# Layer A's head outputs: scaling issued one step later, their transposes in one PSUM bank, v's transposes in the projections' three

## The chip, the cores and the metric

One core of a Trainium2 chip runs the whole program. The metric is the device time of one execution in microseconds (us); of the kernel before, three runs are at hand, and the median is given. The profile comes from a further execution of the same program.

The engines are TensorE (PE in the profile, with its weight loads as PEld), VectorE (DVE), ScalarE (ACT), GpSimd (POOL) and SyncE (SP), which issues the DMAs. TensorE writes its results into PSUM, a small memory with eight banks; the other engines read them from there.

## The reference, cut to what matters

The reference is one inference step of a two-layer decoder trunk on a prompt of 1024 tokens and on 8 sample tokens with a state of their own, all in float32. Layer B (a gated MLP over chunks) is not touched by the change. Layer A is a gated linear recurrence with 8 heads, keys of 128 and values of 256:

```python
proj = h @ w_in
q, f, i, z = jnp.split(proj, [D_MODEL, 2 * D_MODEL, 2 * D_MODEL + D_INNER], axis=-1)
q = jax.nn.silu(q)
logf = jnp.logaddexp(jnp.log(lbh), jnp.log1p(-lbh) + jax.nn.log_sigmoid(f))
k = -jnp.expm1(logf)
o, S = hgrn2_chunkwise(q, k, v=i, logf, s0)     # S_t = diag(f_t) S_{t-1} + k_t v_t^T,  o_t = S_t^T q_t
o = rmsnorm(o, g_norm).reshape(B, L, D_INNER)   # per head, over its 256 values
return (o * jax.nn.silu(z)) @ w_out, S
```

The change concerns the line with `rmsnorm` and the product with `silu(z)`: each head's output `o` comes out with tokens on the partitions, is scaled there by one number for each token, is transposed, and is multiplied by the gate.

## The kernel before

**The work.** The 1032 tokens lie in three chunks of 384, 384 and 264 columns (`W`; the last 8 columns of the third are the sample tokens). A product in float32 is made of three matmuls of shorter operands (lines L230, L231 and L232: high by high, low by high, high by low). A projection (`proj`) of one chunk to 128 outputs is 24 such matmuls into one bank, `ps_proj`. Layer A runs from about 200 to 765 us of the span; most of it is the loop over 8 heads.

For each head h, `head_proj` runs the projections f (three chunks, `fk`), q (three chunks, `qq`: ScalarE makes the sigmoid `sg` at L618, VectorE multiplies it with the projection into `qk` at L619), and v (two halves of 128 outputs by three chunks; ScalarE copies each to `vf` at L720). The last head projects its gate z as well; the other heads' gates were computed earlier and are read back as `zs`.

**The steps.** TensorE executes in the order in which the program is written. Beside the projections stand generators that a counter drives: `tk.tick()` is called in the middle and at the end of each projection and runs whatever has come due; `yield 4` in a generator means "go on four ticks later". A tick is thus half a projection of TensorE's work, about 2 us. The generators of a head are:

- `v_token_major`: transposes v's copy (`pt_v`, three transposes at L763) and splits it into a high part `vh` and a low part `vl` (L226, VectorE);
- `decay` (for each chunk): products of the forget gates on VectorE (L821 to L852), small matmuls (L802), and the transposes of k (`pt_k`, L866), which are split into `kh` and `kl`;
- `recur`: for each 128 tokens the matmuls into `pd` and `po`, the new state `S` (L919) with its parts `Sh` and `Sl`, and `out_sum`: `on` is the copy of the output (L881), and its sum of squares follows at L882;
- `finish` (for each chunk): `out_scale` adds the epsilon (`ss_e`, L888, VectorE) and takes the power -1/2 on GpSimd (`rsq`, L239); ScalarE scales the two or three `on` tiles of the chunk (L940); `OD[0]`, that is 4, ticks later TensorE transposes them (`pt_o`, L894), and VectorE multiplies each by the gate into `oz` (L947);
- `sample`: the sample tokens' states are updated (L981, L982), their outputs are summed into `pos` (L989), and they go the same way as `finish`: scaling at L995, `OD[1]` ticks, transposes (L998, issued at L894), and the product with the gate at L1003.

What a head begins, the next head's first 30 us finish: the output transposes of head h's chunks stand between the projections of head h+1.

The engines other than TensorE don't execute in written order. A scheduler sets their order when the program is built, and moves ahead what stands under `tc.high_priority`. In `finish` the product L947 stands under it, the scaling L940 doesn't.

**The banks.** The tiles in PSUM take a bank by their tag. Tag "mm" has three banks in rotation; "pt" has one. A tile that takes a bank waits until the last reader of the tile that held it is done. Before the change:

- "mm": `ps_proj`, `pt_k`, `pos`, the outputs' transposes `pt_o` of heads 0 to 6, and the sample's transposes of all heads;
- "pt": v's transposes `pt_v`, and the outputs' transposes `pt_o` of the last head;
- one bank each: `po` (tag "po"), `pD` (tag "pA"), `pC`, `pd`.

The functions that the change touches, and what calls them:

## Time and profile before

| | |
|---|---|
| median of 3 runs | 1887.39 us (1887.23 to 1890.06) |
| the profiled execution | 1887.56 us, span 1885.8 us |
| mean granted TensorE clock | 0.991 |
| TensorE busy | 1829.3 us, 97% of the span |
| VectorE busy | 1363.0 us, 72% |
| ScalarE busy | 895.5 us, 47% |
| GpSimd busy | 406.0 us, 22% |
| layer A's heads, 200 to 765 us: TensorE, VectorE, ScalarE, GpSimd busy | 536.37, 452.52, 325.25, 66.99 us of 565 |

The rows of the timeline read: start in us, duration in us, engine, line, operation, output and inputs with their sizes, the number of instructions that the row groups, and in brackets the idle time of the engine just ahead of it with what released it. Where a row groups several instructions, its duration runs from the first one's start to the last one's end. The rows of the waits read: waiting engine, tile and line, then the releaser, then total us, number of waits, the longest one. The rows of the windows give, for each stretch, its length, the busy time of PE, PEld, DVE, ACT and POOL (number of instructions in brackets), then the granted clock, the DMAs' share and their GB/s.

### The profile page before, as it was taken

Reading aid. Unit: us, or ns where it says so; the run is one execution under the profiler, and the core shown is the slowest. Engines: PE = TensorE matmul, PEld = TensorE weight load, DVE = VectorE, ACT = ScalarE, POOL = GpSimd, SP = SyncE. Lnnn points to the kernel's source line nnn. Section 1 sums busy time; section 2 is a strip of 40 time slices with the busy share of each in tenths; the row PEclk is TensorE's granted clock in tenths of the full one; section 3 lists DMA queues with packets and bytes.
Section 4 is the critical chain, followed back from the end, with each engine's and each line's share of the span. In section 5 each row is a group of like instructions: output and inputs, shape, how many; then the busy total and the mean of one; then the engine's idle time right before and its main releaser. Section 6 shows DMA issues by size and latency. Waiting matters only on the chain.

```text
span 1885.8 us, 37107 instructions
## 1 busy us (share of the span) xinstructions
PE 1829.3 (97%) x14458; PEld 1793.3 (95%) x14458; DVE 1363.0 (72%) x2760; ACT 895.5 (47%) x1905; POOL 406.0 (22%) x407
## 2 busy tenths in 40 slices
PE   8999999999999989999999999999999999999997
PEld 7999999998989988999999999999999998999997
DVE  6766788779778767678665855577777878777744
ACT  6533365556556546435344544433444345445342
POOL 4000011011111101000233333244544452000222
PEclk9999999999999989999999999999999999999999
DMA  6233334345444246954343343323334546953223
GB/s 218 78 111 104 110 117 126 115 135 168 157 127 128 86 138 193 309 175 134 95 138 112 115 143 90 101 79 109 117 112 156 180 132 195 305 177 113 72 91 113
DMA packets 164560, 258.11 MB, mean 137 GB/s; under 512 B 16096, under 2 KB 136864, under 8 KB 163360
## 3 DMA queue, kind: packets, MB, share of 16 engines
q1 hardware_dynamic: 164384, 255.74, 42.8%
q8 instruction: 113, 1.85, 0.4%
q14 instruction: 63, 0.52, 0.1%
HBM read 182.88 MB, written 72.80 MB: 136 GB/s over the span
## 4 chain that ended last, share of the span: by engine, by line
PE 72%; DVE 15%; DMA 5%; ACT 3%; issue 3%; POOL 2%; SPq 1%; DVEq 0%; POOLq 0%; ACTq 0%
PE ps_proj L230 17%; PE ps_proj L231 17%; PE ps_proj L232 17%; PE ps_d L230 3%; PE ps_d L232 2%; PE ps_d L231 2%; PE ps_o L230 2%; PE ps_o L231 2%; PE ps_o L232 2%; DMA vb<-vd 1%; DVE wlo L152 1%; POOL rsq L239 1%; DVE S L982 1%; PE psp L1513 1%; DVE M L821 1%
## 5 line engine op out<-in xcount | busy, mean ns | idle before, releaser
L230 PE MATMUL ps_proj<-bh,whi 128*128 128x264 f32 (+1 forms) x2248 | 718.6, 320 | 14.7 <-DVE qk L619 13.3
L231 PE MATMUL ps_proj<-bl,whi 128*128 128x264 f32 (+1 forms) x2248 | 703.2, 313 | 5.3 <-DVE bl L226 2.7
L232 PE MATMUL ps_proj<-bh,wlo 128*128 128x264 f32 (+1 forms) x2248 | 702.5, 313 | 1.2 <-DVE wlo L152 1.2
L230 PEld LDWEIGHTS ps_proj<-bh,whi 128*128 128x128 f32 x2248 | 425.6, 189 | 18.5 <-DVE qk L619 14.7
L231 PEld LDWEIGHTS ps_proj<-bl,whi 128*128 128x128 f32 x2248 | 426.1, 190 | 8.9 <-DVE bl L226 5.5
L232 PEld LDWEIGHTS ps_proj<-bh,wlo 128*128 128x128 f32 x2248 | 425.0, 189 | 2.1 <-DVE wlo L152 2.1
L152 DVE TENSOR_TENSOR wlo<-wstg,whi 128x1024 fp32r<-128x1024 f32 x148 | 184.9, 1249 | 114.2 <-ACT whi L151 113.7
L151 ACT CAST whi<-wstg 128x1024 fp32r<-128x1024 f32 x148 | 155.3, 1049 | 140.4 <-PE ps_proj L231 118.1
L151 ACT CAST shi<-ssum 128x512 fp32r<-128x512 f32 x152 | 94.1, 622 | 190.7 <-PE ps_proj L231 90.5
L152 DVE TENSOR_TENSOR slo<-ssum,shi 128x512 fp32r<-128x512 f32 x152 | 112.0, 739 | 10.4 <-ACT shi L151 10.0
L239 POOL TENSOR_TENSOR rsq<-rms_e,mhalf 128x3 f32<-128x3 f32 x15 | 17.8, 1188 | 360.1 <-DVE rms_e L284 360.1
L230 PE MATMUL ps_proj<-xmh,shi 128*128 128x384 f32 x244 | 83.2, 341 | 2.4 <-DVE sg L1529 1.3
L232 PE MATMUL ps_proj<-xmh,slo 128*128 128x384 f32 x244 | 81.7, 335 | 0.0
L231 PE MATMUL ps_proj<-xml,shi 128*128 128x384 f32 x244 | 81.7, 335 | 0.0
L852 DVE TENSOR_TENSOR qk<-qk,t 128x384 f32<-128x384 f32 (+1 forms) x144 | 74.0, 517 | 8.5 <-PE pC L802 7.3
L230 PE MATMUL ps_o<-bh,whi 128*128 128x384 f32 (+1 forms) x232 | 73.2, 316 | 0.0
L231 PE MATMUL ps_o<-bl,whi 128*128 128x384 f32 (+1 forms) x232 | 72.7, 313 | 0.0
L232 PE MATMUL ps_o<-bh,wlo 128*128 128x384 f32 (+1 forms) x232 | 72.7, 313 | 0.0
L1522 POOL TENSOR_TENSOR s<-s,u 128x384 f32<-128x384 f32 (+1 forms) x48 | 54.2, 1130 | 71.3 <-DVE s L1516 70.7
L1261 DVE TENSOR_TENSOR tmp<-tmp,pj 128x384 f32<-128x384 f32 (+1 forms) x48 | 25.6, 533 | 56.0 <-ACT tmp L1260 52.4
L239 POOL TENSOR_TENSOR rsq<-ss_e,mhalf 128x3 f32<-128x3 f32 (+2 forms) x32 | 27.8, 868 | 172.9 <-DVE ss_e L888 134.9
L266 POOL TENSOR_TENSOR ssq<-ssq,tmp 128x384 f32<-128x384 f32 (+1 forms) x36 | 34.2, 951 | 108.1 <-ACT tmp L265 108.1
(376 smaller groups left out, 4148.1 us busy)
## 6 DMA issues: line engine op xcount, KB each, us to landing
wstg<-in_wina SPq DMA_DIRECT2D x48, 512.0 KB, 3.9
wstg<-in_winb SPq DMA_DIRECT2D x48, 512.0 KB, 4.1
pj<-ppd SPq DMA_DIRECT2D x16, 516.0 KB, 4.8
S<-in_st SPq DMA_DIRECT2D x16, 512.0 KB, 4.7
vb<-vd SPq DMA_DIRECT2D x16, 512.0 KB, 4.9
out_so_s<-S SPq DMA_DIRECT2D x16, 512.0 KB, 3.5
wstg<-in_wouta SPq DMA_DIRECT2D x16, 512.0 KB, 3.7
wstg<-in_wgate SPq DMA_DIRECT2D x16, 512.0 KB, 3.7
```

What stands on the lines that cost most here:

```text
L151: A.copy(hi, src)
L152: V.tensor_tensor(lo, src, hi.bitcast(F32), ALU.subtract)
L230: PE.matmul(ps, wh, xh, start=first, stop=False, skip_group_check=more)
L231: PE.matmul(ps, wh, xl, start=False, stop=False, skip_group_check=more)
L232: PE.matmul(ps, wl, xh, start=False, stop=last, skip_group_check=more)
L239: G.tensor_tensor(y, e, mhalf[:, :n], ALU.pow)
L266: eng.tensor_tensor(ssq, ssq, sq[:, :w], ALU.add)
L821: V.reciprocal(xv[:, :, 0:4], yv[:, :, 0:4])
L852: V.tensor_tensor(lev, lev, t2.rearrange("p two (n o) -> p two n o", o=1).broadcast_to([P, 2, n, lv]), ALU.mult)
L982: V.scalar_tensor_tensor(S0[:, c, :], vb[:, c, :], qs[:, 1, b:b + 1], S0[:, c, :], ALU.mult, ALU.add)
L1261: V.tensor_tensor(gt[:, :w], gt[:, :w], pj[:, OFF[c]:OFF[c] + w], ALU.mult)
L1522: G.tensor_tensor(s[:, :w], s[:, :w], us[mm, c][:, :w], ALU.mult)
```

## The change

`v_token_major` takes its bank by the tag "mm" and no longer by "pt". `finish` takes "pt" for the outputs' transposes in all heads. In `finish` and in `sample` a tick is put between `out_scale` and the scaling, and the pause behind the scaling is one tick shorter, so that the transposes come due at the same tick as before. The sample's transposes keep "mm".

```diff
-        pt = pp.tile([P, 3, P], F32, name="pt_v", tag="pt", bufs=1)
+        pt = pp.tile([P, 3, P], F32, name="pt_v", tag="mm", bufs=3)
...
         y = out_scale(ss[:, :n], n)
+        yield 1
         for i in range(n):
             A.activation(ons[i], ons[i], AF.Copy, scale=y[:, i:i + 1])
-        yield OD[0]
+        yield OD[0] - 1
...
-            pt = out_transpose(ons[i], "mm" if h < NH - 1 else "pt")
+            pt = out_transpose(ons[i], "pt")
...
         y = out_scale(ss, 1)
+        yield 1
         A.activation(on, on, AF.Copy, scale=y)
-        yield OD[1]
+        yield OD[1] - 1
```

Line numbers grow by one from L939 on and by two from L996 on. In the built program TensorE's matmuls and transposes stand in the same order as before, and GpSimd's order is the same too. What changes on TensorE is for what the instructions wait. On ScalarE, VectorE and SP some instructions change places in the heads; behind the heads nothing moves.

In the rows of the built order that follow, a row is one instruction, or several alike with their count; the brackets name the engine for which it waits. First TensorE at the head start of head 6 (about 597 us), before: the last matmuls of the sample's sums `pos`, the transposes of head 5's first outputs, and q's projection of the third chunk.

```order
L989 MATMUL pos<-S_7268,qm 32x256 [waits DVE_49]
L894 MATMUL pt_o<-ident,on 128x128 [waits DVE_49]
L894 MATMUL pt_o<-ident,on 128x128
L230 MATMUL ps_proj<-bh_138,whi 128x264 [waits DVE_49]
L231 MATMUL ps_proj<-bl_141,whi 128x264
L232 MATMUL ps_proj<-bh_138,wlo 128x264
```

And with the change:

```order
L990 MATMUL pos<-S_7268,qm 32x256 [waits DVE_49]
L894 MATMUL pt_o<-ident,on 128x128 x2
L230 MATMUL ps_proj<-bh_138,whi 128x264 [waits DVE_49]
L231 MATMUL ps_proj<-bl_141,whi 128x264
L232 MATMUL ps_proj<-bh_138,wlo 128x264
```

No row moved. The first transposes wait for nothing more of their own, and the projection's wait for VectorE is now for an earlier product of the same kind: it was for L619 of q's second chunk and is for L619 of q's first one.

Some 8 us later on TensorE, the end of that projection, the third transposes of the same outputs, and the next projection (v's first), before:

```order
L231 MATMUL ps_proj<-bl_141,whi 128x264
L232 MATMUL ps_proj<-bh_138,wlo 128x264
L894 MATMUL pt_o<-ident,on 128x128 [waits Activation_49]
L894 MATMUL pt_o<-ident,on 128x128
L230 MATMUL ps_proj<-bh_136,whi 128x384 [waits DVE_49]
```

And with the change:

```order
L231 MATMUL ps_proj<-bl_141,whi 128x264
L232 MATMUL ps_proj<-bh_138,wlo 128x264
L894 MATMUL pt_o<-ident,on 128x128 [waits DVE_49]
L894 MATMUL pt_o<-ident,on 128x128
L230 MATMUL ps_proj<-bh_136,whi 128x384
```

Again the rows stand where they stood. The third transposes now wait for VectorE, that is for L947 of the second transposes, which held the same bank.

ScalarE at the same head start, about 602 to 608 us, before. `S_8285` is a half of the sample's states of head 6.

```order
L995 ACTIVATE on<-on,rsq_8183 128x256
L844 COPY qk_8339<-qk 128x384
L981 ACTIVATE S_8285<-S_8285,qs 128x256
L225 CAST Sh<-S 128x256
L881 COPY on<-po 128x256
L882 ACTIVATE po,ss<-po 128x256
L844 COPY qk_8344<-qk 128x384
L981 ACTIVATE S_8285<-S_8285,qs 128x256
L618 ACTIVATE sg<-ps_proj 128x264
L151 CAST whi<-wstg 128x1024
```

And with the change:

```order
L997 ACTIVATE on<-on,rsq_8183 128x256
L844 COPY qk_8339<-qk 128x384
L982 ACTIVATE S_8285<-S_8285,qs 128x256
L881 COPY on<-po 128x256
L225 CAST Sh<-S 128x256
L882 ACTIVATE po,ss<-po 128x256
L844 COPY qk_8344<-qk 128x384
L618 ACTIVATE sg<-ps_proj 128x264
L151 CAST whi<-wstg 128x1024
```

One scaling of the states moved from ahead of L618 to behind it, and the copy `on` moved ahead of the cast `Sh`. The scaling of the sample's output (L995, now L997) stands in the same place, and so do the rows ahead of it, with the three scalings of the first outputs around L618 of q's second chunk:

```order
L882 ACTIVATE po,ss<-po 128x256
L941 ACTIVATE on<-on,rsq_8234 128x256 x2
L618 ACTIVATE sg<-ps_proj 128x384
L941 ACTIVATE on<-on,rsq_8234 128x256
L839 COPY k_8332<-qk 128x384
```

With L940 for L941 these are also the rows of before; none of them moved.

Last, TensorE in the middle of head 6 (about 628 us), where head 5's last outputs, a k chunk, head 5's sample outputs and a v chunk are transposed one behind the other, before:

```order
L894 MATMUL pt_o<-ident,on 128x128 [waits Activation_49]
L894 MATMUL pt_o<-ident,on 128x128
L866 MATMUL pt_k<-ident,qk 128x128 [waits DVE_49]
L866 MATMUL pt_k<-ident,qk 128x128 x2
L894 MATMUL pt_o<-ident,on 128x128 [waits DVE_49,PE_49]
L894 MATMUL pt_o<-ident,on 128x128
L763 MATMUL pt_v<-ident,vf 128x128 x3
```

And with the change:

```order
L894 MATMUL pt_o<-ident,on 128x128 [waits Activation_49]
L894 MATMUL pt_o<-ident,on 128x128
L866 MATMUL pt_k<-ident,qk 128x128 [waits DVE_49,PE_49]
L866 MATMUL pt_k<-ident,qk 128x128 x2
L894 MATMUL pt_o<-ident,on 128x128 [waits DVE_49]
L894 MATMUL pt_o<-ident,on 128x128
L763 MATMUL pt_v<-ident,vf 128x128 [waits DVE_49,PE_49]
L763 MATMUL pt_v<-ident,vf 128x128 x2
```

The rows keep their order; v's transposes have taken over a wait for a bank.

## The prediction

> **What bounds the kernel now.** I read the page first, then who waited for whom in layer A's heads (200 to 765 us), then the timelines of those waits.

> ```profile
> span 1885.8 us, 37107 instructions
> ...
> PE 1829.3 (97%) x14458; PEld 1793.3 (95%) x14458; DVE 1363.0 (72%) x2760; ACT 895.5 (47%) x1905; POOL 406.0 (22%) x407
> ...
> PE 72%; DVE 15%; DMA 5%; ACT 3%; issue 3%; POOL 2%; SPq 1%; DVEq 0%; POOLq 0%; ACTq 0%
> ```

> TensorE is busy for 97% of the span and has most of the chain that ended last. The change takes no matmul away, so only TensorE's waits, and its clock, can pay. Of the waits in the heads (total, times, longest):

> ```profile
> PE ps_proj L230 <- DVE qk L619: 13.3, 6, 3.3
> PE pt_o L894 <- DVE oz L1003: 4.4, 6, 1.1
> PE pt_v L763 <- DVE vl L226: 2.3, 1, 2.3
> ```

> The first is one wait in each of the heads 2 to 7, the second one in each of the same heads, the third one in head 7. All three are waits for a bank. Here is the first, in head 2 and in head 6:

> ```profile
> 328.39 0.44 PE L894 MATMUL pt_o<-ident,on 128*128 128x128 f32 x2
> 330.59 0.39 PE L230 MATMUL ps_proj<-bh,whi 128*128 128x264 f32 x1 [1.76 <-DVE qk L619]
> ...
> 334.90 0.38 PE L894 MATMUL pt_o<-ident,on 128*128 128x128 f32 x2
> ...
> 597.44 0.44 PE L894 MATMUL pt_o<-ident,on 128*128 128x128 f32 x2
> 599.79 0.40 PE L230 MATMUL ps_proj<-bh,whi 128*128 128x264 f32 x1 [1.91 <-DVE qk L619]
> ...
> 605.63 0.38 PE L894 MATMUL pt_o<-ident,on 128*128 128x128 f32 x2
> ```

> The three rows of a head are the first output transposes of the previous head's chunk 0, q's projection of chunk 2, and the third transposes. That projection wants one of three banks: the sample's sums hold one, the transposes just took the second, and the third still holds q's chunk 1, until VectorE has multiplied it (L619). VectorE and ScalarE at the same place:

> ```profile
> 333.73 0.42 DVE L947 TENSOR_TENSOR oz<-pt_o,zs 128x256 f32<-128x256 f32 x1
> ...
> 593.80 0.49 DVE L619 TENSOR_TENSOR qk<-ps_proj,sg 128x384 f32<-128x384 f32 x1
> 599.18 0.56 DVE L619 TENSOR_TENSOR qk<-ps_proj,sg 128x384 f32<-128x384 f32 x1 [0.87 <-ACT sg L618]
> 599.65 0.41 DVE L947 TENSOR_TENSOR oz<-pt_o,zs 128x256 f32<-128x256 f32 x1
> ...
> 603.29 0.48 DVE L919 SCALAR_TENSOR_TENSOR S<-S,t,pd 128x256 f32<-128x256 f32 x1 [1.30 <-PE pd L232]
> ...
> 604.37 0.42 DVE L947 TENSOR_TENSOR oz<-pt_o,zs 128x256 f32<-128x256 f32 x1
> ```

> ```profile
> 597.87 0.91 ACT L940 ACTIVATE on<-on,rsq 128x256 f32<-128x256 f32 x2 [1.62 <-POOL rsq L239]
> 598.68 0.47 ACT L618 ACTIVATE sg<-ps_proj 128x384 f32<-128x384 f32 x1
> ```

> The multiplication is late because its sigmoid (L618) stands behind two scalings (L940), which wait for GpSimd. Last, stretches of 3.41 us with TensorE's busy time and its granted clock (PEclk, behind POOL's column):

> ```profile
> 326.97:330.39 3.42, 1.86 (x21) 0.79 (x19) 2.48 (x7) 1.80 (x6) 1.16 (x1) 1.00 0.21 55
> ...
> 531.77:535.18 3.41, 3.17 (x14) 3.17 (x15) 2.34 (x7) 2.62 (x8) 0.60 (x1) 0.50 0.35 121
> 596.62:600.03 3.41, 1.50 (x20) 0.70 (x13) 2.47 (x7) 2.17 (x6) 1.16 (x1) 1.00 0.40 117
> 600.03:603.45 3.42, 3.42 (x17) 3.42 (x17) 2.02 (x7) 2.14 (x7) 0.60 (x1) 0.50 0.58 190
> ...
> 699.02:702.43 3.41, 2.17 (x8) 2.18 (x9) 3.04 (x9) 0.85 (x2) 0.00 (x0) 0.50 0.59 189
> 702.43:705.85 3.42, 3.42 (x14) 3.42 (x13) 0.63 (x2) 0.48 (x1) 0.00 (x0) 0.50 0.72 233
> ```

> **The change, part by part.**

> *The scaling one step later.* In the built order the scalings stand where they stood, also around L618: ScalarE's order is made by a scheduler, not by the step. What moves in the heads is one scaling of the sample's state (L981), from before L618 of chunk 2 to behind an L882, and an `on` copy ahead of `Sh`. Both are worth under half a microsecond on ScalarE and are hidden by its idle time before L940. In the last head's tail scalings do move behind casts; bounds there are plus and minus 1 us, I take 0. L619 is thus not earlier.

> *The head start.* The outputs' transposes leave the three banks; the projection then waits for q's chunk 0, which the L619 of 593.80 has read by 594.29, 5.5 us before the projection runs. The wait of 13.3 us in all is gone. But the three transposes now share a bank, so the second waits for the first's L947 and the third for the second's. The second: in head 6 TensorE would come at 600.5, L947 ends at 599.65 + 0.41 = 600.06: no wait. The third: in head 2 TensorE would come at 334.90 - 1.76 = 333.14, but L947 ends at 334.15, plus 0.06 as between L619's end and the projection: 334.21. VectorE is not faster than before (its queue behind L619 has no gap in head 2), so 334.90 - 334.21 = 0.7 us is the gain of a head, whatever its wait was: L947 comes a fixed time behind L619. Six heads: 4.2. What was 1.76 becomes a wait of 1.07 one place later.

> *The clock.* Head 6 needs 605.63 - 597.44 = 8.19 us for the stretch that head 2 does in 6.51; 0.15 of that is the longer wait, 1.53 the half clock. VectorE's wait of 1.30 for `pd` is this loss seen from its side, so it vanishes with it. Three heads: 4.6. New waits of some 1.1 us leave more than 1.86 of 3.41 us busy. In head 5 (the 3.3 us) VectorE is late by itself and 3.3 - 0.7 = 2.6 us remain, there a half clock stays as likely as not, and head 4 may trip one: minus 0.9.

> *v's first transposes* (pt_v) wait for a copy on ScalarE, whose queue has no gap ahead of it:

> ```profile
> 612.21 0.46 ACT L720 COPY vf<-ps_proj 128x384 f32<-128x384 f32 x1
> ```
> ```profile
> 613.21 0.49 PE L763 MATMUL pt_v<-ident,vf 128*128 128x128 f32 x3
> ```

> TensorE has 0.5 us in hand there and comes up to 2.2 earlier; ScalarE's queue follows by about 1.6. Four heads at 0.1 to 0.2: minus 0.5.

> *The sample's transposes* (L1003 reads them) stay in the three banks, and so does pt_v now. In head 6, and in head 7:

> ```profile
> 629.16 0.41 PE L894 MATMUL pt_o<-ident,on 128*128 128x128 f32 x2 [0.66 <-DVE oz L1003]
> 629.41 0.38 PE L763 MATMUL pt_v<-ident,vf 128*128 128x128 f32 x2
> ...
> 695.91 0.49 PE L866 MATMUL pt_k<-ident,qk 128*128 128x128 f32 x3
> 697.51 0.41 PE L894 MATMUL pt_o<-ident,on 128*128 128x128 f32 x2 [1.11 <-DVE oz L1003]
> 700.25 0.90 PE L763 MATMUL pt_v<-ident,vf 128*128 128x128 f32 x3 [2.33 <-DVE vl L226]
> ```
> ```profile
> 628.80 0.21 DVE L1003 TENSOR_TENSOR oz<-pt_o,zs 128x8 f32<-128x8 f32 x2
> ...
> 697.20 0.17 DVE L1003 TENSOR_TENSOR oz<-pt_o,zs 128x8 f32<-128x8 f32 x2
> ...
> 697.66 0.55 DVE L226 TENSOR_TENSOR kl<-pt_k,kh 128x384 fp32r<-128x384 f32 x1
> ```

> In heads 2 to 6 pt_o no longer waits 0.66, but pt_v behind it takes the sample's bank: it would come at 628.75 and L1003 ends at 629.01 + 0.06: 0.32 are waited, 0.34 gained, 1.7 in five heads. In head 7 the k transposes take that bank: they wait from 695.91 to 697.43. Then pt_v needs `kl`, which ends 2.3 us after pt_k's start, with less queue ahead of it some 1.85: 699.3 against 700.25, 0.95 gained. The 5.59 us at half clock lost 2.8; with 2.6 us of waits left I give back 1.0 of it, 1.8 gained.

> *A new wait.* At the head's end a projection of head 7 takes the bank of v's last transposes:

> ```profile
> 715.24 0.37 PE L230 MATMUL ps_proj<-bh,whi 128*128 128x264 f32 x1
> ```
> ```profile
> 715.97 0.42 DVE L226 TENSOR_TENSOR vl<-pt_v,vh 128x256 fp32r<-128x256 f32 x1
> ```

> That is minus 1.2. In the other heads the same `vl` ends just in time, or stands further ahead in the new order.

> Sum: 4.2 + 4.6 - 0.9 - 0.5 + 1.7 + 0.95 + 1.8 - 1.2 = 10.6. The profiled execution took 1887.56 us (span 1885.8, the rest lies around it), the median of the runs is 1887.39. After the heads TensorE's order, waits and banks' readers are the same, so the gain is carried to the end: **1877.0 us**. Moved DMAs on SP (`zs` behind a weight load and the state's store) load gates for the next head, some 60 us ahead of use: 0. Its own range runs from 1871 to 1883: head starts between 0.4 and 1.2 each, head 7 between minus 1 and plus 4.

> **The rivals.**

> *All waits vanish and none comes instead*, because VectorE, let go earlier, runs ahead: 13.3 + 4.6 + 4.4 + 2.3 + 2.8 = 27.4, so 1860. Against it: VectorE has no gap ahead of head 2's L947, and L940 still waits for GpSimd.

> *Each new wait halves the clock* in all six heads: 6 x 1.53 = 9.2 lost against 11.5 gained without my clock term: 1885.3, no measurable change. For it: the stretches lie at fixed times, and a wait's place in them shifts. Against it: 1.76 us did not trip it.

> ```profile
> L152 DVE TENSOR_TENSOR wlo<-wstg,whi 128x1024 fp32r<-128x1024 f32 x148 | 184.9, 1249 | 114.2 <-ACT whi L151 113.7
> ```

> *Slower: the single bank serialises.* The third transposes wait for an L947 that slips behind one more weight row on VectorE (1.2 us, L152's mean), and the longer wait then halves the clock: 6 x (1.2 + 1.53) = 16.4 against 11.5: 1892.5. It decides from 11.5 / 6 = 1.9 us lost per head. [...] Against it: L947's place in VectorE's order is unchanged up to the third.

> **How the numbers follow.** Forecast 0.68; all vanish 0.10; clock cancels it, or the change does nothing, 0.14; slower 0.08. About 0.2% (3.8 us) can be told from no change. Faster by more: 0.78; within: 0.14; slower: 0.08. The range takes in the whole lower forecast, part of the full gain and the cancelling case: 1867 to 1885.5.

> **What would show it.** Right: the wait of ps_proj for L619 at the head starts gone; a wait of pt_o for L947 of about 1 us, six times, in its place; no half clock in heads 6 and 7; pt_v waiting 0.3 for L1003 and pt_k 1.5 once. Wrong: pt_o without waits (the full gain), or L947 later than 5.8 us after a head's first transposes, or half clocks in heads 2 and 3.

## The result, and the profile after

The changed kernel took 1874.88 us in the median of 4 runs, the kernel before 1887.81 us in its 4: a ratio of 0.9928, with a 95% interval of 0.9911 to 0.9945. A second set on another occasion gave 1874.62 us against 1888.93 us, 0.9922 (0.9907 to 0.9938). So the change saves some 13 to 14 us; 10.6 were forecast (1877.0 us). The profiled execution took 1875.28 us, 12.3 less than that of before.

Single executions of one and the same program scatter by several us here (before: 1884.15 to 1896.47 us in 29 runs), in part for a reason that `e_step` shows below, so traces are compared place by place and times by medians.

From the page after, the span, the busy times and the chain that ended last by engine:

```profile
span 1873.5 us, 37132 instructions
...
PE 1823.9 (97%) x14458; PEld 1787.9 (95%) x14458; DVE 1366.9 (73%) x2760; ACT 895.0 (48%) x1905; POOL 404.4 (22%) x407
...
PE 70%; DVE 16%; DMA 6%; ACT 3%; issue 3%; POOL 2%; SPq 0%; DVEq 0%; POOLq 0%; ACTq 0%
```

TensorE is busy for 5.4 us less with the same matmuls: that part is mostly the clock, since in layer A's heads the trace of before has six stretches of 3.41 us at half clock and that of after two (and one more in layer B). The rest, some 7 us, is idle time that is gone. TensorE's waits in the heads after (total us, times, longest):

```profile
PE pt_o L894 <- DVE oz L948: 9.1, 8, 1.4
PE pt_v L763 <- DVE oz L1005: 2.3, 5, 0.5
PE pt_k L866 <- DVE qk L619: 2.2, 1, 2.2
PE ps_proj L230 <- DVE vl L226: 2.1, 1, 2.1
...
PE pt_k L866 <- DVE oz L1005: 1.5, 1, 1.5
PE pt_v L763 <- DVE kl L226: 1.1, 1, 1.1
```

The wait of a projection for L619 at the head starts (13.3 us) is gone. In its place stands the wait of `pt_o` for the product L948 (L947 before) that empties the single bank, 9.1 us in eight. Seven of them, 8.3 us, are at head starts; the eighth, 0.82 us, is in the last head, where the single bank was used before too and 0.9 us were waited. The rows with L1005 and `kl` are the smaller waits that v's and k's transposes took over. The one of `pt_k` for L619 is in head 1 and was there before (1.9 us); that of the projection for `vl`, in head 7, is new. TensorE at the starts of heads 2, 5 and 6 after:

```profile
327.01 0.44 PE L894 MATMUL pt_o<-ident,on 128*128 128x128 f32 x2
...
332.83 0.44 PE L894 MATMUL pt_o<-ident,on 128*128 128x128 f32 x2 [1.17 <-DVE oz L948]
...
528.73 0.44 PE L894 MATMUL pt_o<-ident,on 128*128 128x128 f32 x2 [1.24 <-DVE oz L948]
532.01 0.44 PE L894 MATMUL pt_o<-ident,on 128*128 128x128 f32 x2 [1.36 <-DVE oz L948]
...
591.51 0.44 PE L894 MATMUL pt_o<-ident,on 128*128 128x128 f32 x2
...
597.46 0.44 PE L894 MATMUL pt_o<-ident,on 128*128 128x128 f32 x2 [1.31 <-DVE oz L948]
```

In head 2 the way from the first to the third transposes took 334.90 - 328.39 = 6.51 us before and takes 332.83 - 327.01 = 5.82 us now; in head 6 it was 8.19 and is 5.95. VectorE at head 2's start after, with the first two products:

```profile
328.62 0.56 DVE L619 TENSOR_TENSOR qk<-ps_proj,sg 128x384 f32<-128x384 f32 x1 [0.88 <-ACT sg L618]
329.09 0.41 DVE L948 TENSOR_TENSOR oz<-pt_o,zs 128x256 f32<-128x256 f32 x1
...
332.36 0.42 DVE L948 TENSOR_TENSOR oz<-pt_o,zs 128x256 f32<-128x256 f32 x1
```

L619 at the same place in the trace of before; its second product started at 333.73 us:

```profile
329.97 0.56 DVE L619 TENSOR_TENSOR qk<-ps_proj,sg 128x384 f32<-128x384 f32 x1 [0.87 <-ACT sg L618]
```

L619 still waits for the sigmoid, and the second product still starts 3.7 to 3.8 us behind it. The clock, in stretches of 3.41 us at head 6's start and in head 7 (length, busy times, then the granted clock behind POOL's column):

```profile
595.58:598.99 3.41, 2.10 (x15) 1.89 (x14) 3.35 (x10) 3.41 (x10) 0.00 (x0) 1.00 0.11 39
598.99:602.40 3.41, 3.41 (x24) 3.41 (x23) 3.41 (x10) 3.41 (x10) 0.20 (x1) 1.00 0.50 141
701.40:704.81 3.41, 1.29 (x11) 1.20 (x10) 3.41 (x9) 2.08 (x8) 0.00 (x0) 1.00 0.48 137
704.81:708.22 3.41, 3.41 (x18) 3.41 (x17) 1.53 (x4) 0.95 (x4) 0.00 (x0) 0.50 0.78 247
```

A wait of 1.31 us leaves TensorE busy for 2.10 us of the stretch, and the next one runs at full clock. The wait for `vl` in head 7 leaves 1.29 us, and the next one runs at half.

Where the 12.3 us came from, by the starts of the same TensorE instruction in both traces:

| Part of the program | its end, as the start of one instruction, before and after | gained in it, us | forecast, us |
|---|---|---|---|
| up to head 2's first `pt_o` | 328.39, 327.01 | 1.4 | 0 |
| heads 2 to 6 and head 7's start | 695.69, 685.22 | 9.1 | 9.1 (4.2 + 4.6 - 0.9 - 0.5 + 1.7) |
| the rest of head 7 | 754.79, 743.03 | 1.3 | 1.55 (0.95 + 1.8 - 1.2) |
| layer B | 1877.77, 1865.41 | 0.6 | 0 |

### The profile page after: what moved, and what is told of

The parts are those of the page before. It is cut to its first block, busy times and chain, and to the rows that moved or that the text cites. A ratio compares the mean times of both kernels' runs of the same rounds, so it can differ in the third digit from the quotient of the medians.

```text
span 1873.5 us, 37132 instructions
## 1 busy us (share of the span) xinstructions
PE 1823.9 (97%) x14458; PEld 1787.9 (95%) x14458; DVE 1366.9 (73%) x2760; ACT 895.0 (48%) x1905; POOL 404.4 (22%) x407
## 3 DMA queue, kind: packets, MB, share of 16 engines
q8 instruction: 113, 1.85, 0.4%
## 4 chain that ended last, share of the span: by engine, by line
PE 70%; DVE 16%; DMA 6%; ACT 3%; issue 3%; POOL 2%; SPq 0%; DVEq 0%; POOLq 0%; ACTq 0%
PE ps_proj L230 16%; PE ps_proj L232 16%; PE ps_proj L231 16%; PE ps_o L230 2%; PE ps_d L230 2%; PE ps_o L231 2%; PE ps_o L232 2%; PE ps_d L232 2%; PE ps_d L231 2%; DMA vb<-vd 2%; POOL rsq L239 1%; DVE wlo L152 1%; DVE S L983 1%; PE psp L1515 1%; DVE M L821 1%
## 5 line engine op out<-in xcount | busy, mean ns | idle before, releaser
L230 PE MATMUL ps_proj<-bh,whi 128*128 128x264 f32 (+1 forms) x2248 | 716.7, 319 | 3.5 <-DVE vl L226 2.1
L232 PE MATMUL ps_proj<-bh,wlo 128*128 128x264 f32 (+1 forms) x2248 | 700.8, 312 | 1.2 <-DVE wlo L152 1.2
L230 PEld LDWEIGHTS ps_proj<-bh,whi 128*128 128x128 f32 x2248 | 424.1, 189 | 6.0 <-issue 2.7
L232 PEld LDWEIGHTS ps_proj<-bh,wlo 128*128 128x128 f32 x2248 | 423.1, 188 | 2.1 <-DVE wlo L152 2.1
L152 DVE TENSOR_TENSOR wlo<-wstg,whi 128x1024 fp32r<-128x1024 f32 x148 | 184.1, 1244 | 114.2 <-ACT whi L151 113.7
L151 ACT CAST whi<-wstg 128x1024 fp32r<-128x1024 f32 x148 | 155.4, 1050 | 141.5 <-PE ps_proj L231 121.6
L151 ACT CAST shi<-ssum 128x512 fp32r<-128x512 f32 x152 | 94.1, 621 | 189.2 <-PE ps_proj L231 91.8
L152 DVE TENSOR_TENSOR slo<-ssum,shi 128x512 fp32r<-128x512 f32 x152 | 114.1, 753 | 9.3 <-ACT shi L151 8.8
L239 POOL TENSOR_TENSOR rsq<-rms_e,mhalf 128x3 f32<-128x3 f32 x15 | 17.8, 1189 | 362.5 <-DVE rms_e L284 362.5
L230 PE MATMUL ps_proj<-xmh,shi 128*128 128x384 f32 x244 | 82.9, 340 | 0.4 <-DVE u L497 0.4
L232 PE MATMUL ps_proj<-xmh,slo 128*128 128x384 f32 x244 | 81.7, 335 | 0.0
L230 PE MATMUL ps_o<-bh,whi 128*128 128x384 f32 (+1 forms) x232 | 73.2, 316 | 0.0
L232 PE MATMUL ps_o<-bh,wlo 128*128 128x384 f32 (+1 forms) x232 | 72.7, 313 | 0.0
L239 POOL TENSOR_TENSOR rsq<-ss_e,mhalf 128x3 f32<-128x3 f32 (+2 forms) x32 | 28.3, 884 | 177.7 <-DVE ss_e L888 155.4
```

The costliest lines, as they stand in the source:

```text
L151: A.copy(hi, src)
L152: V.tensor_tensor(lo, src, hi.bitcast(F32), ALU.subtract)
L230: PE.matmul(ps, wh, xh, start=first, stop=False, skip_group_check=more)
L232: PE.matmul(ps, wl, xh, start=False, stop=last, skip_group_check=more)
L239: G.tensor_tensor(y, e, mhalf[:, :n], ALU.pow)
```

## The experiments

Every experiment is told by its edit, what was expected, what came, and what follows.

**The parts alone.** First the step without the banks, `e_step`:

```diff
         y = out_scale(ss[:, :n], n)
+        yield 1
...
-        yield OD[0]
+        yield OD[0] - 1
```

and the same in `sample`.

> The step alone: the scalings are issued one tick later, all tiles keep the banks of before. Theory (the banks do it): 1887.5, between 1886 and 1889, since the scheduler puts every instruction of every engine where it stood; the wait of ps_proj for L619 stays at 13.3 us in six. Rival (the later scaling lets L618 and L619 go earlier at the head starts): 1884 or less, with that wait at 10 us or less.

It took 1889.15 us against 1887.52 us, a ratio of 1.0007 (0.9996 to 1.0018): no change, with a median 0.15 us above the range that was stated. In both traces TensorE's matmuls, VectorE, ScalarE and GpSimd run in the same order, so the step by itself brings nothing. As it is the program of before, its trace is a second one of that program. TensorE at head 4's start, in this run and then in that of before; behind them the stretches around it, in the same order:

```profile
459.89 0.44 PE L894 MATMUL pt_o<-ident,on 128*128 128x128 f32 x2
462.85 0.59 PE L230 MATMUL ps_proj<-bh,whi 128*128 128x264 f32 x1 [2.52 <-DVE qk L619]
```
```profile
461.38 0.44 PE L894 MATMUL pt_o<-ident,on 128*128 128x128 f32 x2
464.32 0.39 PE L230 MATMUL ps_proj<-bh,whi 128*128 128x264 f32 x1 [2.50 <-DVE qk L619]
```
```profile
458.70:462.11 3.41, 1.63 (x20) 0.62 (x18) 2.64 (x9) 1.93 (x8) 1.12 (x1) 1.00 0.28 88
462.11:465.52 3.41, 2.67 (x12) 2.67 (x13) 2.62 (x7) 2.86 (x10) 0.79 (x1) 0.50 0.66 220
```
```profile
460.09:463.50 3.41, 1.73 (x21) 0.66 (x19) 2.72 (x9) 1.93 (x7) 1.12 (x1) 1.00 0.24 71
463.50:466.92 3.42, 2.60 (x21) 2.60 (x22) 3.12 (x9) 2.88 (x10) 0.79 (x1) 1.00 0.71 236
```

The wait is the same (2.52 us; 2.50 before). What differs is where the stretches begin: 1.19 us ahead of the first transposes here, 1.29 us ahead in the run of before. With 1.63 us of work in its stretch the clock falls, with 1.73 us it does not. From the first to the third transposes head 4 takes 469.88 - 459.89 = 9.99 us here and 468.62 - 461.38 = 7.24 us in the run of before. From head 1 on this execution has nine half stretches (two of them in head 4), that of before six, and it is 2.9 us longer (1890.46 us).

Next the outputs' transposes alone in the single bank, v's there too, `e_pto`:

```diff
-            pt = out_transpose(ons[i], "mm" if h < NH - 1 else "pt")
+            pt = out_transpose(ons[i], "pt")
```

> Only the outputs' transposes go to the single bank; v's transposes stay there too, and the scaling is as before. Theory: the head starts gain as with the whole change (some 9 us: 4.3 by the shorter wait, 4.6 by the clock), but outputs and v now wait for each other in one bank: by the ends of their readers in the trace of before some 0.6 + 1.3 + 0.6 us in each of the heads 2 to 6, 5 in head 1, 5 in head 7, together some 18 to 20. So slower than before: 1898, between 1892 and 1906. Rival (taking the outputs' transposes out of the three banks is all that counts, and v's tag is immaterial): 1875 to 1880.

It took 1896.42 us, a ratio of 1.0051 (1.0039 to 1.0064): slower, as expected. TensorE's waits in it:

```profile
PE pt_v L763 <- DVE oz L947: 13.5, 15, 1.4
PE pt_o L894 <- DVE vl L226: 13.0, 7, 4.7
PE pt_o L894 <- DVE oz L947: 9.1, 8, 1.4
```

The third row is the one that the whole change has, to the tenth. The first two are the price of one bank for two users.

Then v's transposes alone in the three banks, `e_ptv`:

```diff
-        pt = pp.tile([P, 3, P], F32, name="pt_v", tag="pt", bufs=1)
+        pt = pp.tile([P, 3, P], F32, name="pt_v", tag="mm", bufs=3)
```

> Only v's transposes go to the projections' three banks; the outputs' transposes stay there too, and the scaling is as before. Theory: the wait of ps_proj for L619 at the head starts and its half clocks stay, and the three banks have one more user: new waits of a projection for vf (0.8 us) and of pt_v for kl (1.1) in each of the heads 2 to 6, some more in heads 1 and 7: slower than before, 1896, between 1889 and 1902. Rival (v's transposes were held up by their single bank, and freeing them is a good part of the gain): 1883 or less.

It took 1887.28 us, a ratio of 0.9998 (0.9986 to 1.0010): no change, where I had expected 1896. Its waits:

```profile
PE ps_proj L230 <- DVE qk L619: 11.5, 6, 2.0
PE ps_proj L230 <- ACT vf L720: 4.8, 7, 1.0
PE pt_v L763 <- DVE kl L226: 3.8, 5, 0.8
```

The new waits that I had named are there, 8.6 us. But I had left the old ones standing: the waits of `pt_o` for L1003 (4.4 us) are gone, and one of `pt_k` for L1003 (0.4) came; that of `pt_v` for `vl` in head 7 (2.3) is gone, and the head starts wait 1.8 less. Waits that I had not named came too: `pt_o` for L947 has 3.3 us (0.9 before) and for `kl` 1.2. The half clocks did not stay either: from head 2 to head 7 this trace has one half stretch where that of before has five. How these terms add up to no change, the runs don't show. So neither bank move pays alone, and together they gain 13 us: the outputs may leave the three banks only if v leaves the single one.

**The clock by itself.** `e_fill` is the kernel before with work put into the wait:

```diff
             pt = out_transpose(ons[i], "mm" if h < NH - 1 else "pt")
+            if c == 0 and i == 0 and 0 < h < NH - 1:
+                ft = pp.tile([P, 384], F32, name="ft", tag="pt", bufs=1)
+                for _ in range(7):
+                    PE.matmul(ft, hh[0][:, 0, :P], hh[0][:, 0, :], start=True, stop=True)
```

> The kernel before with seven more matmuls of 128x384 (some 1.3 us, their result is not read) at each of the six head starts, between the first output transposes and the projection that waits there. The wait for L619 stays, TensorE is only busier while it lasts. Theory (a stretch of 3.41 us with little work halves the clock in the next one, and three of the head starts pay 1.5 us for it): no half clock at the head starts of heads 5, 6 and 7, 1883, between 1881 and 1885.5. Rival (the slow stretch behind the wait is VectorE's own lateness, or the clock falls whatever TensorE does there): 1887 or more, by up to 6 x 1.3 = 8 us if the matmuls don't fit into the wait.

It took 1885.51 us, at the slow edge of the range that was stated: a ratio of 0.9983 (0.9971 to 0.9995), 3.2 us less by the ratio and 2.0 by the medians. TensorE at head 6's start in its trace:

```profile
596.43 0.44 PE L894 MATMUL pt_o<-ident,on 128*128 128x128 f32 x2
596.62 1.48 PE L949 MATMUL ft<-bh 128*128 128x384 f32 x7
598.78 0.39 PE L230 MATMUL ps_proj<-bh,whi 128*128 128x264 f32 x1 [0.68 <-DVE qk L619]
...
603.09 0.38 PE L894 MATMUL pt_o<-ident,on 128*128 128x128 f32 x2
```

The projection starts 2.35 us behind the first transposes, as before (599.79 - 597.44), so L619 is as late as it was. But no head start from head 2 on has a half clock in this trace, and the third transposes come 603.09 - 596.43 = 6.66 us behind the first ones, where it was 8.19: the 1.53 us that the prediction had put down to the half clock. Head 7 gains the same. Seven matmuls that nobody needs make the kernel faster: the clock's part is one of its own, 2 to 3 us over the runs. It is less than the 4.6 us of the three starts, since some 0.5 us is lost again behind each start, where the next projection now waits (0.23 us in head 6). The profiled execution took 1882.71 us, 4.9 less than that of before, but 2.3 of these lie ahead of head 2, where no matmul was added. How much comes from VectorE's and ScalarE's orders, which moved in places, stays open.

**What is left at the head starts.** `e_alt` is the changed kernel with the second transposes of a head's first chunk back in the three banks; every engine's order stays:

```diff
-            pt = out_transpose(ons[i], "pt")
+            pt = out_transpose(ons[i], "mm" if i == 1 and c == 0 and h < NH - 1 else "pt")
```

> The changed kernel, but the second of the three output transposes of a head's first chunk takes one of the projections' three banks (heads 0 to 6), so that the third waits only for the first's L948. No instruction of any engine changes its place. Theory (the wait of about 1.2 us that is left at each head start is for the single bank alone, and VectorE can follow): the six waits of the third transposes, 7.1 us in all, are gone, 1868, between 1866 and 1870. Rival (VectorE is what sets the pace there, and the time comes back as waits of the next projections or of v's transposes): 1872 or more.

It took 1875.17 us (ratio to before 0.9934, 0.9919 to 0.9950): no gain over the changed kernel. The third transposes do come without a wait, 4.5 us behind the first ones. Nine us later the gain is given back. TensorE's largest wait in this run, and TensorE and ScalarE in its head 2:

```profile
PE pt_v L763 <- ACT vf L720: 8.6, 7, 1.6
```

```profile
327.08 0.44 PE L894 MATMUL pt_o<-ident,on 128*128 128x128 f32 x2
...
331.58 0.38 PE L894 MATMUL pt_o<-ident,on 128*128 128x128 f32 x2
340.32 0.55 PE L763 MATMUL pt_v<-ident,vf 128*128 128x128 f32 x3 [1.00 <-ACT vf L720]
```
```profile
338.99 0.91 ACT L941 ACTIVATE on<-on,rsq 128x256 f32<-128x256 f32 x2 [0.62 <-POOL rsq L239]
339.81 0.46 ACT L720 COPY vf<-ps_proj 128x384 f32<-128x384 f32 x1
```

`pt_v` now waits for its copy `vf`, which stands behind two scalings that wait for GpSimd. The expected 1868 us were a miss. The next engine in line was ScalarE, and not VectorE, as the rival had it; the rival's time was right.

`e_late` takes the scalings out of the sigmoid's way instead; `tc.issue_after` places what stands under it behind the named instruction, here the last sigmoid:

```diff
-            A.activation(sg[:, :w], ps[:, :w], AF.Sigmoid)
+            last["sg"] = A.activation(sg[:, :w], ps[:, :w], AF.Sigmoid)
...
-        for i in range(n):
-            A.activation(ons[i], ons[i], AF.Copy, scale=y[:, i:i + 1])
+        with tc.issue_after(last["sg"].ins) if h < NH - 1 else ExitStack():
+            for i in range(n):
+                A.activation(ons[i], ons[i], AF.Copy, scale=y[:, i:i + 1])
```

> The changed kernel, with the scalings of a chunk's outputs (L941) held behind the sigmoid of q (L618) on ScalarE; the banks are those of the changed kernel. Theory (L619 is late because its sigmoid stands behind scalings that wait for GpSimd): L619 of q's second chunk no longer waits for ScalarE (0.87 us in each head), and the waits of the third transposes shrink by as much, 5 us in all: 1870, between 1868 and 1872.5. Rival (VectorE's other work sets when L619 and L948 come, the sigmoid was hidden): 1874 to 1876.

It took 1869.06 us, a ratio of 0.9908 (0.9891 to 0.9924). VectorE at head 2's start, and the wait that is left:

```profile
324.97 0.55 DVE L619 TENSOR_TENSOR qk<-ps_proj,sg 128x384 f32<-128x384 f32 x1
```
```profile
PE pt_o L894 <- DVE oz L949: 3.7, 7, 1.2
```

L619 has no idle time ahead of it any more, and 9.1 us became 3.7. The prediction's account of why L619 is late is thereby shown. The time has a second source, though: the 2.2 us that `pt_k` waited for an L619 in head 1 are gone too.

`e_latebank` does the same to the kernel before, with none of the change's banks (edit as in `e_late`, with the step).

> The kernel before, all its banks as they were, with the scalings of a chunk's outputs held behind the sigmoid of q on ScalarE, as in e_late. Theory (the projection waits for L619 because the scalings, which wait for GpSimd, stand ahead of its sigmoid): L619 comes 0.9 us earlier at each head start, the waits of ps_proj for it fall from 13.3 to some 8 us, and two or three of the half clocks behind them go: 1879, between 1876 and 1882. Rival (the banks alone decide; VectorE is busy up to L619 anyway): 1885 or more.

It took 1873.07 us, a ratio of 0.9922 (0.9905 to 0.9939), the same as the change brings, and more than I had expected. TensorE's waits for L619 in it, and the start of head 2:

```profile
PE ps_proj L230 <- DVE qk L619: 7.4, 6, 2.2
```
```profile
323.58 0.44 PE L894 MATMUL pt_o<-ident,on 128*128 128x128 f32 x2
324.82 0.39 PE L230 MATMUL ps_proj<-bh,whi 128*128 128x264 f32 x1 [0.80 <-DVE qk L619]
```

The head starts came out as reckoned: 7.4 us are left of 13.3, and the half clocks at the starts of heads 6 and 7 are gone (head 5's stays). What I had missed lies in part in head 1: there `pt_k` waited 1.9 us for an L619 too, with a half clock behind it, and both are gone in this trace (in that of `e_late` the wait is gone and a half clock stays in head 1). By place, this execution gains 4.8 us up to head 2's first transposes, 1.4 of them ahead of layer A. So the change treats a symptom: the time comes either with another bank for the transposes or with an earlier sigmoid.

The changed kernel was run once more, as `after_again`:

> The changed kernel once more, for a closer interval and beside e_latebank on the same chip: 1875, ratio to before 0.993. Its profiled execution counts the half clocks again: if they depend on where an execution falls in a free-running grid of 3.41 us, as the two traces so far suggest, the ones outside of head 7 come at other places or not at all.

The repeat gave 1874.62 us (above). Its profiled execution has a half clock in head 7 at 706.05 us, as the first trace has at 704.81, and one at 1654.95 us in layer B, where the first has one at 1585.45. Both also have one in head 1, at 262.31 and at 261.08 us. So the one in layer B moved, and those in heads 1 and 7 stayed, which is half of what I had expected.

**Toward a better kernel.** `e_v7` is the changed kernel with the price in head 7 taken back:

```diff
-        pt = pp.tile([P, 3, P], F32, name="pt_v", tag="mm", bufs=3)
+        own = h == NH - 1 and m == 1 and c == 2
+        pt = pp.tile([P, 3, P], F32, name="pt_v", tag="pt" if own else "mm", bufs=1 if own else 3)
```

> The changed kernel, but in the last head the last transposes of v go to the single bank again, so that the projection behind them no longer waits for vl. Theory (that wait, 2.1 us, and the half clock behind it, 1.7, are the price that the change pays in head 7): 1871.5, between 1870 and 1873.5. Rival (VectorE is late there by itself, and kl, which stands behind vl, is waited for next): 1874 to 1876.

1872.89 us, a ratio of 0.9917 (0.9899 to 0.9935); the wait for `vl` is 0.2 us, and the trace has no half clock in head 7. The medians say 2 us, but the intervals of this kernel and of the changed one overlap, so the gain isn't shown.

`e_altlate` puts `e_alt` and `e_late` together.

> The second output transposes in the projections' banks (as in e_alt) and the scalings behind the sigmoid (as in e_late), together. Theory (behind the head start ScalarE's copy vf is the next to be waited for, and the scalings now stand in front of it): the 3.7 us of waits that e_late left at the third transposes come back at pt_v for vf, so no better than e_late: 1869, between 1867 and 1871. Rival (the two gains add): 1865 or less.

1868.98 us, 0.9891 (0.9871 to 0.9912): no better than `e_late` alone, with `pt_v` waiting 5.3 us for `vf` in five waits. `e_altstate` is `e_alt` with the scalings of the sample's states held back:

```diff
-                    A.copy(vf[:, :w], ps[:, :w])
+                    last["vf"] = A.copy(vf[:, :w], ps[:, :w])
...
-                A.activation(S0[:, c, :], S0[:, c, :], AF.Copy, scale=qs[:, 0, b:b + 1])
+                with tc.issue_after(last["vf"].ins):
+                    A.activation(S0[:, c, :], S0[:, c, :], AF.Copy, scale=qs[:, 0, b:b + 1])
```

> As e_alt, and the eight scalings of the sample's states (L982) of each head are held behind a copy vf near the head's end, so that they no longer stand in ScalarE's queue at the head start; nobody needs them before the next head. Theory (in e_alt the gain came back because ScalarE's queue, the scalings of the states in it, makes vf late): pt_v's waits for vf fall from 8.6 to 2 us or less, 1868, between 1866 and 1871. Rival (VectorE's queue holds the heads' pace): 1873 or more, with another wait in the place.

1869.83 us, 0.9896 (0.9876 to 0.9915): the time that was expected, by half the mechanism. ScalarE in head 2 of this run:

```profile
334.91 0.38 ACT L882 ACTIVATE po<-po 128x256 f32<-128x256 f32 x1
335.21 0.19 ACT L882 ACTIVATION_READ_ACCUMULATOR po<-po 128x1 f32 x1
337.81 0.91 ACT L941 ACTIVATE on<-on,rsq 128x256 f32<-128x256 f32 x2 [2.42 <-POOL rsq L239]
338.63 0.46 ACT L720 COPY vf<-ps_proj 128x384 f32<-128x384 f32 x1
```

ScalarE is idle for 2.42 us now, and `vf` stands behind the scalings all the same: the waits for it fell to 4.5 us, not to 2. Here it isn't ScalarE's load but its order that holds `vf`. Meanwhile TensorE's waits for `vl` rose from 1.8 to 4.4 us, so the gain isn't that of `vf`, and where it lies stays open.

`e_all7` has all four: `e_alt`, `e_late`, the states and `e_v7`.

> All of it: the second output transposes in the projections' banks, the scalings of the outputs behind the sigmoid, the scalings of the states near the head's end, and v's last transposes of the last head in the single bank (as in e_v7). Theory (ScalarE's order is what the head starts wait for): the 5 to 6 us of e_late, 2 to 3 more of the waits it left, and the 2 to 4 of e_v7: 1863.5, between 1860 and 1867. Rival (VectorE holds the pace): 1869 or more.

1862.53 us in the median of 4 (1859.61 to 1863.53), a ratio to before of 0.9857 (0.9835 to 0.9879): better than both kernels by a clear margin, and as reckoned. In the window of the heads TensorE is busy for 552.49 of 565 us, where it was 536.37 before (the window is fixed in time, and so holds 5640 matmuls here and 5489 before):

```profile
200.00:765.00 565.00, 552.49 (x5640) 532.84 (x5640) 470.27 (x1148) 333.29 (x873) 68.29 (x99) 1.00 0.47 149
```

## Why the prediction was right, point by point

- *The scaling one step later: 0.* Right, and stronger than I had it: `e_step` executes as the program of before does. The moves on ScalarE and VectorE that I put under this head don't come from the step alone.
- *The head start: 0.7 us each.* Right. From a head's first transposes to its third ones the six starts gained 0.69, 0.66, 1.02, 1.98, 2.24 and 2.22 us; less 1.53 for each of the three half stretches that is 4.2 us, as forecast. The second product starts 332.36 - 328.62 = 3.74 us behind L619, where it was 333.73 - 329.97 = 3.76. "The second: no wait" failed in the two heads where VectorE is late by itself (in head 5 L619 starts 527.79 - 524.54 = 3.25 us behind the first transposes, in head 2 1.61): in head 5 it waits 1.24 us (above), in head 4 0.81, put down to L888. The sum of both waits in head 5, 2.60 us, is the 2.6 that I had named. Of the signs of being wrong, "L947 later than 5.8 us" showed in one head: in head 5 the second product starts 531.54 - 524.54 = 7.00 us behind the first transposes, in the others 5.35 to 5.75.
- *The clock: 4.6, less 0.9.* The three half stretches went, and no new wait at a head start cost one in the two traces of the changed kernel, so the 0.9 that I gave back was not needed. The sign "no half clock in heads 6 and 7" held for their starts; head 7 has one further on, under another wait (below). The waits of 1.91 us and of 2.12 us had a half stretch behind them, in the traces of before (at 600.03 us) and after (at 704.81 us). The stretches do not keep step with the heads: one begins 1.19 us ahead of head 4's first transposes in `e_step`, and 1.29 us ahead of them in the trace of before.
- *The sample's transposes: 1.7.* Too much. `pt_v` waits 0.45 us for L1005, not 0.32 (five waits, 2.3 us), so a head gained 0.2 us at most, some 0.8 us in the five.
- *v's first transposes: minus 0.5.* Hardly there: `pt_v` waits for `vf` in none of these heads after the change, since the third transposes' wait comes ahead of it and covers it. `e_alt` shows that the reason given was right: without that wait, the one for `vf` comes, with 8.6 us. That heads 2 to 6 with head 7's start came out at the very 9.1 us that were forecast is therefore luck in part: the 1.7 for the sample's transposes was 0.9 too much, the 0.9 given back for the clock offsets it, and some 0.5 us of small losses behind the head starts stand where this 0.5 was forecast.
- *Head 7.* `pt_k` waits 1.5 us for L1005 (forecast 1.5), and `pt_v` comes at 688.89 us, 3.67 behind the sample's transposes (685.22), where it was 4.56 before: 0.89 gained, 0.95 forecast. The new wait for `vl` was put at 1.2 us and is 2.12, and with the half clock behind it (the stretch at 704.81) it costs 3.9, which I had not seen. Against that, the gain ahead of it was 3.5 us and not 2.75, since both half stretches at 699 went, and 1.7 more came in the last head's tail, where I had taken 0. The near hit of this sum (1.3 for 1.55) is misses that offset each other.
- *The other 2 us* lie ahead of head 2 and in layer B, where I had taken 0. In `e_step`, without the banks, the first part is 1.4 us shorter than in the trace of before as well, and in layer B the program is the same: scatter.
- The rivals: a full gain needed an earlier L619, which the change doesn't bring (`e_late` does). The new waits at the head starts did not halve the clock. The single bank did not serialise the transposes beyond one wait per head, and two in heads 4 and 5.

Two readings in the part on the change were wrong: the three scalings around L618 belong to the second chunk's outputs and not to the first ones, and among the transposes at about 628 us the first pair is the sample's, the last `pt_o` the chunk's. No term of the sum rests on either.

## What to carry to other kernels

When TensorE waits for a bank, ask why its last reader is late before giving the tile another bank: here a sigmoid stood behind scalings that waited 1.62 us for GpSimd and that nobody needed for 15 us (scaled from 327.30 us on, transposed from 342.92 us on), and VectorE's product L619, which needs the sigmoid, waited 0.88 us for it. Moving users between banks may pay only as a set: each half of this change alone was neutral or slower. And a gain at one wait is real only if the next engine in line can follow: in `e_alt` it was given back nine microseconds later.

## What the runs showed of the hardware

Work that nobody needs, put into a wait, made the kernel faster (`e_fill`, 0.9983), since in these traces TensorE's clock was at half for 3.41 us behind a stretch of that length with too little work: in that of before, 1.50 us of work from 596.62 us on, then 0.50 of the clock from 600.03 us on. The half stretches of that trace from head 1 on begin at 262.12, 531.77, 600.03, 668.30 and 699.02 us (the last is followed by a second one at once), which lie 79, 20, 20 and 9 times 3.413 us apart ((699.02 - 262.12) / 128). The bound isn't sharp: 1.63 us of work was too little at head 4 of `e_step`, 1.73 us was enough at the same place in the trace of before; elsewhere 1.51 us was enough (before, at 210.92 us), 1.83 us too little (`e_ptv`, at 263.13 us), and near the program's start even 2.46 us (after, at 22.14 us). In a stretch at half clock 2.67 us of work did not bring the full clock back for the next one (`e_step`, at 462.11 us). What decides between these stays open. Where the stretches begin differs from execution to execution (1.29 us and 1.19 us ahead of head 4's first transposes in the trace of before and in `e_step`), and with the same instructions in the same order the first of these had six half stretches from head 1 on and the second nine, 2.9 us apart in time.
